# Transposes as a queue of single steps between projection matmuls, in place of groups of three to eight

## The chip, the cores and the metric

The kernel runs on one core of one Trainium2 chip. The metric is the device time of one execution in microseconds (us); the time of a kernel is the median of several executions. A difference of about 0.2% (4.6 us) is the least that a measurement of this kernel can tell from none.

## What is computed

A trunk of two decoder layers over 256 tokens of width 2048, in float32. Layer 0 mixes tokens with an mLSTM (four heads, value width 512), layer 1 with FoX attention (sixteen heads of width 128). Each layer then has a SwiGLU feed-forward block of inner width 5632, and a root-mean-square norm stands before each block and at the end:

```python
for layer in range(DEPTH):
    sh1, sc1, g1, sh2, sc2, g2 = split(silu(c) @ ada_w[layer] + ada_b[layer], 6)
    h = rms_norm(x, norm_mix_w[layer]) * (1.0 + sc1) + sh1
    y = mlstm_mixer(h, ...) if layer % 2 == 0 else fox_mixer(h, ...)
    x = x + g1 * y
    h = rms_norm(x, norm_ffn_w[layer]) * (1.0 + sc2) + sh2
    g, u = split(h @ w_gate_up[layer], 2)
    x = x + g2 * ((silu(g) * u) @ w_down[layer])
return rms_norm(x, final_norm_w)
```

## The kernel before

All weights are streamed from HBM once. `fetch` (L252) brings four blocks of 128 rows by 512 columns (1 MB) into one of five `raw` buffers. `split` (L257) makes of each half of it two float32r tiles: ScalarE casts `hi` (L263), VectorE computes the remainder `lo` (L264); `hi` and `lo` have four buffers each, and a half feeds two contraction steps. The activations are split in the same way, so a product is the sum of three float32r matmuls of 512 columns: `mm_t` (L287) does these three for one half of the tokens (L290, L291, L292), and `mm_a` calls it for both token halves. One fetch in `group_a` is therefore 8 calls of `mm_t`, 24 matmuls. Where the result is wanted with the tokens along the free axis, `mm_b` (L270) does the same with two matmuls, 512 columns (L273) and 256 columns (L276).

Some results come out with tokens on the partitions and are needed the other way round. TensorE turns them in blocks of 128 x 128: a transpose is a matmul with the block as the stationary operand and an identity matrix as the moving one. The places are `turned` (L342, four blocks into one PSUM bank, used for the SwiGLU output, L1093, and for the mLSTM queries and keys), `Norm.turn` (L478, four blocks of the normed residual, L485), `weights_t` (L889, three blocks of attention weights, L893), `emit` (L963, mLSTM output, L970) and `x_block` (L692, L695). After each group ScalarE and VectorE read the PSUM bank: for SwiGLU a cast (L1095) and a subtraction (L1096). The banks for this come from the pool `aux`, which has two.

What is not a projection waits in a list `steps` of jobs (transposes with their readers, attention scores, the mixing of a head). After each fetch `tick` (L242) calls `drain(adv)`, which settles outstanding PSUM copies and runs the next one or two jobs as a whole; then `bg` emits tiles of the adaLN modulation (`ada_tile`, L191): a DMA of 1 MB and one VectorE instruction over 2048 columns (L195). A `drain()` without a count runs all jobs that are left; one stands at the end of each of the two parts of a feed-forward block (6 and 5 groups of columns), before the down projection reads the activations. `carry_on` (L592) runs `Norm.rest` for one quarter of the columns ahead of a fetch.

The program is recorded in this order, and a scheduler then sets the order on each engine, except in the first part and in `bridge`, where it is by hand.

Of the kernel before, what the change touches and what calls it, by code (L numbers as in the profile page):

```python
# [31 lines left out]
def kernel(  # L32
# [201 lines left out]
    steps = []  # L234
    later = []

# [4 lines left out]
    def drain(n=None):  # L241
        if steps:  # L242
            settle()
        for _ in range(len(steps) if n is None else min(n, len(steps))):
            steps.pop(0)()
# [41 lines left out]
    def mm_t(ps, hi, lo, act, t, first, last):  # L287
# [4 lines left out]
        nc.tensor.matmul(ps, b, hi, start=False, stop=last, skip_group_check=True)  # L292

# [4 lines left out]
    def group_b(w, nk, c0, act, evac, bgn, adv=1):  # L298
        banks = [bank() for _ in range(4)]
        for k in range(0, nk, 4):  # L300
            ws = load_w(w, k, 4, c0)
            for m in range(4):
                cols = slice(m * P, (m + 1) * P)
                for j, (hi, lo) in enumerate(ws):
                    mm_b(
                        banks[m], hi[:, cols], lo[:, cols], act(k + j), k + j == 0, k + j == nk - 1
                    )
                if k + 4 == nk:
                    evac(m, banks[m])
# [33 lines left out]
    def turned(src, i):  # L343
        ps = abank()
        for j in range(2):
            for t in range(2):
# [3 lines left out]
                )  # L350
        return ps.rearrange("p (k t) -> p k t", t=T)
# [108 lines left out]
    class Norm:  # L460
# [62 lines left out]
        def rest(self, t, q):  # L523
            self.turn(t, q)
            self.affine(t, q)
# [66 lines left out]
    def carry_on(w2, hb, norm, rate):  # L592
        todo = [(0, 2), (1, 2), (0, 3), (1, 3)]

        def each(k):
            if todo:
                norm.rest(*todo.pop(0))
# [3 lines left out]
        for k in (4, 8):  # L601
            for n, (c, banks) in enumerate(hb.items()):
                group_a(w2, c, h_act, rate, ka=k, kb=k + 4, banks=banks, each=each if n < 2 else None)

# [87 lines left out]
    def x_block(t, j):  # L692
        ps = abank()
        for i in range(4):
            nc.tensor.transpose(  # L695
                ps[:, i * P : (i + 1) * P], xT[4 * j + i][:, t * P : (t + 1) * P], ident
            )
        nc.scalar.copy(X[:, t, 512 * j : 512 * (j + 1)], ps)

    ready_sqrt(eps_t)  # L700
    x_block(0, 0)
# [10 lines left out]
    x_block(1, 0)  # L712

    def row_scale():
# [9 lines left out]
        for t in range(2):  # L724
            x_block(t, 1)
# [157 lines left out]
    def act_tile(lst, k):  # L883
        return lst[k // 2][:, k % 2, :]
# [4 lines left out]
    def weights_t(W, WT):  # L889
        ps = abank()  # L890
        for i in range(3):
            cols = slice(i * P, (i + 1) * P)
            nc.tensor.transpose(ps[:, cols], W[:, cols], ident)  # L893
        nc.scalar.copy(WT, ps[:, : 3 * P])

    def mlstm_head(hd, q, k):
# [36 lines left out]
        def flip():  # L933
            weights_t(st["W"], st["WT"])
# [28 lines left out]
        def emit():  # L963
            yt = st["yt"]
            for i in range(2):
                y[2 * hd + i] = new_act()
                ps = abank()
                for j in range(2):
                    for t in range(2):
                        nc.tensor.transpose(  # L970
                            ps[:, j * T + t * P : j * T + (t + 1) * P],
                            yt[:, t, (2 * i + j) * P : (2 * i + j + 1) * P], ident,
                        )
                for j in range(2):
                    c = 4 * hd + 2 * i + j
                    dst = y[2 * hd + i][:, j, :]
                    src = ps[:, j * T : (j + 1) * T]
# [4 lines left out]
                    )  # L982

# [5 lines left out]
    def keep_t(c0, bgn, scale=None, adv=1, layer_w=0):  # L989
        if layer_w == 0:  # L990
# [5 lines left out]
            def flip():  # L996
                for i in range(2):
                    nc.scalar.copy(o[:, 2 * i : 2 * i + 2, :], turned(sp, i))
# [45 lines left out]
    def ffn(layer, begun, norm, rates, nsplit=0, srate=0.0, nxt=None):  # L1044
# [21 lines left out]
        for tq in quarters:  # L1066
            norm.rest(*tq)
# [13 lines left out]
        def swiglu(gr):  # L1081
# [10 lines left out]
            def flip(i):  # L1092
# [245 lines left out]
```

## Time and profile before

| | us |
|---|---|
| median of three runs (2296.80 to 2297.88) | 2297.38 |
| the profiled execution | 2300.83 |
| its span, first to last instruction | 2299.0 |
| PE (TensorE matmul) busy | 2275.4 |
| DVE (VectorE) busy | 1612.9 |
| ACT (ScalarE) busy | 1122.8 |

The granted TensorE clock is 1.00 in every stretch. In a row of the timeline the first number is the start, the second how long the record lasted. Matmuls overlap in the records (one that lasts 0.39 us is followed by the next after 0.23 us), so what a matmul costs is read from the starts: the time from one start to the next is called pitch below. PEld is the load of the stationary operand that each matmul has, in a row of its own. "[0.48 <-DVE ...]" at the end of a row is idle time before it and what ended it.

### The profile page before, as it was taken

Reading aid. Unit: us, or ns where it says so; the run is one execution under the profiler, and the core shown is the slowest. Engines: PE = TensorE matmul, PEld = TensorE weight load, DVE = VectorE, ACT = ScalarE, POOL = GpSimd, SP = SyncE. Lnnn points to the kernel's source line nnn. Section 1 sums busy time; section 2 is a strip of 40 time slices with the busy share of each in tenths; the row PEclk is TensorE's granted clock in tenths of the full one; section 3 lists DMA queues with packets and bytes.
Section 4 is the critical chain, followed back from the end, with each engine's and each line's share of the span. In section 5 each row is a group of like instructions: output and inputs, shape, how many; then the busy total and the mean of one; then the engine's idle time right before and its main releaser. Section 6 shows DMA issues by size and latency. Waiting matters only on the chain.

```text
span 2299.0 us, 26543 instructions
## 1 busy us (share of the span) xinstructions
PE 2275.4 (99%) x10376; PEld 1861.0 (81%) x10376; DVE 1612.9 (70%) x1829; ACT 1122.8 (49%) x1488; POOL 15.6 (1%) x40
## 2 busy tenths in 40 slices
PE   8999999999999999999999999999999999999998
PEld 4777878888888888888878888888888888888886
DVE  5998788878887878865687777777655554544554
ACT  3778664555543344444555444455444433444443
POOL 0000000000000000000000000000000000000000
PEclk9999999999999999999999999999999999999999
DMA  9998989798989889985667878775766555555552
GB/s 348 364 368 320 355 313 362 271 345 325 331 331 336 323 337 337 342 293 188 215 243 285 300 259 288 255 275 186 250 241 222 191 191 198 189 187 195 193 196 105
DMA packets 89090, 623.92 MB, mean 271 GB/s; under 512 B 10034, under 2 KB 10482, under 8 KB 14596
## 3 DMA queue, kind: packets, MB, share of 16 engines
q1 hardware_dynamic: 87552, 617.79, 74.3%
q0 software_dynamic: 1264, 4.29, 0.5%
q8 instruction: 81, 1.33, 0.2%
q14 instruction: 45, 0.37, 0.0%
q10 hardware_dynamic: 148, 0.14, 0.0%
HBM read 620.05 MB, written 2.13 MB: 271 GB/s over the span
## 4 chain that ended last, share of the span: by engine, by line
PE 88%; DVE 6%; DMA 3%; ACT 2%; issue 1%; SPq 0%; ACTq 0%; DVEq 0%
PE mm L292 25%; PE mm L291 25%; PE mm L290 25%; PE mm L273 5%; DVE ada L195 3%; PE mm L276 2%; DVE lo L264 2%; DMA ada<-in_ada_w_dram 2%; PE aux L347 1%; ACT hi L263 1%; DMA raw<-in_w_in_dram 1%; DMA slot<-in_w_in_dram 1%; PE aux L945 0%; PE aux L485 0%; PE aux L1144 0%
## 5 line engine op out<-in xcount | busy, mean ns | idle before, releaser
L264 DVE TENSOR_TENSOR lo<-raw,hi 128x1024 fp32r<-128x1024 f32 x764 | 926.9, 1223 | 556.8 <-ACT hi L263 556.2
L263 ACT CAST hi<-raw 128x1024 fp32r<-128x1024 f32 x764 | 797.1, 1053 | 920.3 <-PE mm L292 816.9
L291 PE MATMUL mm<-lo,hT 128*128 128x512 f32 x1840 | 718.3, 390 | 5.3 <-DVE lo L264 5.3
L290 PE MATMUL mm<-hi,hT 128*128 128x512 f32 x1840 | 719.3, 393 | 0.0
L292 PE MATMUL mm<-hi,hT 128*128 128x512 f32 x1840 | 718.1, 390 | 0.0
L195 DVE SCALAR_TENSOR_TENSOR ada<-ada,cs 128x2048 f32<-128x2048 f32 x192 | 438.9, 2286 | 49.2 <-DMA ada<-in_ada_w_dram 49.2
L291 PEld LDWEIGHTS mm<-lo,hT 128*128 128x128 f32 x1840 | 345.7, 188 | 80.1 <-DVE lo L264 10.2
L292 PEld LDWEIGHTS mm<-hi,hT 128*128 128x128 f32 x1840 | 345.4, 188 | 72.7 <-issue 0.5
L290 PEld LDWEIGHTS mm<-hi,hT 128*128 128x128 f32 x1840 | 345.3, 188 | 70.9 <-ACT hi L263 0.5
L290 PE MATMUL mm<-hi,slot 128*128 128x512 f32 x960 | 375.1, 391 | 0.2 <-ACT slot L978 0.2
L291 PE MATMUL mm<-lo,slot 128*128 128x512 f32 x960 | 374.4, 390 | 0.0
L292 PE MATMUL mm<-hi,slot 128*128 128x512 f32 x960 | 374.4, 391 | 0.0
L290 PEld LDWEIGHTS mm<-hi,slot 128*128 128x128 f32 x960 | 180.3, 188 | 37.7 <-ACT slot L978 0.8
L292 PEld LDWEIGHTS mm<-hi,slot 128*128 128x128 f32 x960 | 180.2, 188 | 37.6 <-issue 0.7
L291 PEld LDWEIGHTS mm<-lo,slot 128*128 128x128 f32 x960 | 180.2, 188 | 37.0
L273 PE MATMUL mm<-hT,hi 128*128 128x512 f32 x512 | 181.7, 402 | 0.6 <-DVE slot L359 0.6
L276 PE MATMUL mm<-hT,lo 128*128 128x256 f32 x512 | 138.3, 280 | 0.0
L273 PEld LDWEIGHTS mm<-hT,hi 128*128 128x128 f32 x512 | 94.4, 188 | 20.5 <-DVE slot L359 0.9
L276 PEld LDWEIGHTS mm<-hT,lo 128*128 128x128 f32 x512 | 96.6, 189 | 3.0
L800 ACT ACTIVATE slot<-mm 128x512 f32<-128x512 f32 x78 | 45.0, 593 | 33.9 <-PE mm L292 31.1
L435 ACT ACTIVATE t<-X 128x512 f32<-128x512 f32 x32 | 20.2, 631 | 39.2 <-DVE X L430 39.2
L1085 ACT ACTIVATE slot<-mm 128x512 f32<-128x512 f32 x44 | 25.4, 598 | 15.0 <-PE mm L292 13.8
(207 smaller groups left out, 980.5 us busy)
## 6 DMA issues: line engine op xcount, KB each, us to landing
ada<-in_ada_w_dram SPq DMA_DIRECT2D x192, 1024.0 KB, 6.5
raw<-in_gate_up_dram SPq DMA_DIRECT2D x176, 1024.0 KB, 4.9
raw<-in_down_dram SPq DMA_DIRECT2D x88, 1024.0 KB, 4.9
raw<-in_fox_in_dram SPq DMA_DIRECT2D x48, 1024.0 KB, 5.0
raw<-in_w_in_dram SPq DMA_DIRECT2D x44, 1024.0 KB, 7.3
raw<-in_w_out_dram SPq DMA_DIRECT2D x16, 1024.0 KB, 5.8
raw<-in_fox_out_dram SPq DMA_DIRECT2D x16, 1024.0 KB, 4.9
slot<-in_w_in_dram SPq DMA_DIRECT2D x16, 256.0 KB, 12.1
```

What stands on the lines that cost most here:

```text
L195: nc.vector.scalar_tensor_tensor(out=raw, in0=raw, scalar=1.0, in1=cs, op0=ALU.mult, op1=ALU.mult, accum_out=acc[layer][:, j : j + 1],)
L263: nc.scalar.copy(hi, raw[:, j : j + 2, :])
L264: nc.vector.tensor_tensor(lo, raw[:, j : j + 2, :], hi.bitcast(F32), op=ALU.subtract)
L273: nc.tensor.matmul(ps, hi, rhs, start=first, stop=last, skip_group_check=True)
L276: nc.tensor.matmul(ps[:, T:], lo, rhs[:, :T], start=False, stop=False, skip_group_check=True)
L290: nc.tensor.matmul(ps, a, hi, start=first, stop=False, skip_group_check=True)
L291: nc.tensor.matmul(ps, a, lo, start=False, stop=False, skip_group_check=True)
L292: nc.tensor.matmul(ps, b, hi, start=False, stop=last, skip_group_check=True)
L347: nc.tensor.transpose(ps[:, j * T + t * P : j * T + (t + 1) * P], src[:, t, (2 * i + j) * P : (2 * i + j + 1) * P], ident,)
L435: nc.scalar.activation(t512(), X[:, t, 512 * i : 512 * (i + 1)], AF.Square, accum_out=self.ss[:, t, i : i + 1],)
L800: nc.scalar.activation(SP[i][:, t, :], banks[t], func)
L1085: nc.scalar.activation(sg[:, t, :], banks[t], AF.Silu)
```

## The change

Jobs become generators. `drain(n)` no longer runs jobs but moves them to a list `active`; `poke()` advances the first of them by one step, and `mm_t` calls it after its three matmuls, `mm_b` after every second pair. Each transpose in `turned`, `weights_t`, `x_block` and `Norm.rest` is followed by a `yield`, so at most one transpose comes between two calls of `mm_t`; the readers of the PSUM bank are emitted one poke after the last transpose. `act_tile` forces jobs to their end when a projection asks for an activation that is not there yet, and for that the lists of activations are filled only when a tile is complete. The `drain()` ahead of the down projection is gone. `emit` uses `turned`. Jobs that are no generators (scores, mix) run whole at one poke. `carry_on` has a `drain()` ahead of each round and at its end. No computation and no transfer is added or removed, and on each engine the counts of instructions by kind are the same.

```diff
@@ -232,17 +232,40 @@
             bg(1.0)
 
     steps = []
+    active = []
     later = []
+
+    def run(f):
+        g = f()
+        if g is not None:
+            yield from g
+
+    def now(g):
+        for _ in g:
+            pass
+
+    def poke():
+        if active and next(active[0], None) is None:
+            active.pop(0)
+
+    def force():
+        if not active:
+            settle()
+            active.append(run(steps.pop(0)))
+        now(active.pop(0))
 
     def settle(n=0):
         while len(later) > n:
             later.pop(0)()
 
     def drain(n=None):
+        if n is None:
+            while active or steps:
+                force()
+            return
         if steps:
             settle()
-        for _ in range(len(steps) if n is None else min(n, len(steps))):
-            steps.pop(0)()
+        active.extend(run(steps.pop(0)) for _ in range(min(n, len(steps))))
 
     def tick(n, adv=1):
         drain(adv)
@@ -290,6 +313,7 @@
         nc.tensor.matmul(ps, a, hi, start=first, stop=False, skip_group_check=True)
         nc.tensor.matmul(ps, a, lo, start=False, stop=False, skip_group_check=True)
         nc.tensor.matmul(ps, b, hi, start=False, stop=last, skip_group_check=True)
+        poke()
 
     def mm_a(ps, hi, lo, act, first, last):
         for t in range(2):
@@ -305,6 +329,8 @@
                     mm_b(
                         banks[m], hi[:, cols], lo[:, cols], act(k + j), k + j == 0, k + j == nk - 1
                     )
+                    if j % 2:
+                        poke()
                 if k + 4 == nk:
                     evac(m, banks[m])
             tick(bgn, adv)
@@ -348,6 +374,7 @@
                     ps[:, j * T + t * P : j * T + (t + 1) * P],
                     src[:, t, (2 * i + j) * P : (2 * i + j + 1) * P], ident,
                 )
+                yield True
         return ps.rearrange("p (k t) -> p k t", t=T)
 
     def total(ps, out, scale=None):
@@ -521,7 +548,13 @@
             self.low(t, q)
 
         def rest(self, t, q):
-            self.turn(t, q)
+            src = self.x[t, q // 2][:, 512 * (q % 2) : 512 * (q % 2) + 512]
+            ps = abank()
+            for j in range(4):
+                cols = slice(j * P, (j + 1) * P)
+                nc.tensor.transpose(ps[:, cols], src[:, cols], ident)
+                yield True
+            self.ps[t, q] = [ps]
             self.affine(t, q)
 
     def bridge(w, row0, nk, c0, act, res, i, norm, w2, heads, rate=0.0):
@@ -594,13 +627,15 @@
 
         def each(k):
             if todo:
-                norm.rest(*todo.pop(0))
+                active.append(norm.rest(*todo.pop(0)))
             if todo:
                 norm.scale(*todo[0])
 
         for k in (4, 8):
+            drain()
             for n, (c, banks) in enumerate(hb.items()):
                 group_a(w2, c, h_act, rate, ka=k, kb=k + 4, banks=banks, each=each if n < 2 else None)
+        drain()
 
     def scratch(n):
         tiles = []
@@ -695,10 +730,11 @@
             nc.tensor.transpose(
                 ps[:, i * P : (i + 1) * P], xT[4 * j + i][:, t * P : (t + 1) * P], ident
             )
+            yield True
         nc.scalar.copy(X[:, t, 512 * j : 512 * (j + 1)], ps)
 
     ready_sqrt(eps_t)
-    x_block(0, 0)
+    now(x_block(0, 0))
     ssb = bank()
     parts = [sq[:, T * i : T * (i + 1)] for i in range(4)] + [s_end]
     for t in range(2):
@@ -709,7 +745,7 @@
             )
     r0 = small([P, 2], "rstd")
     nc.scalar.activation(r0, ssb[:, :2], AF.Sqrt, bias=eps_t, scale=1.0 / D)
-    x_block(1, 0)
+    now(x_block(1, 0))
 
     def row_scale():
         nc.vector.reciprocal(r0, r0)
@@ -722,7 +758,7 @@
         nc.tensor.matmul(ps[:, :T], ones, dg, start=True, stop=True)
         nc.scalar.copy(R, ps[:, :T])
         for t in range(2):
-            x_block(t, 1)
+            now(x_block(t, 1))
 
     w = w_in
     COLS = [2048 + 512 * i for i in range(8)] + [0, 1024, 512, 1536]
@@ -881,6 +917,8 @@
     y = [None] * 8
 
     def act_tile(lst, k):
+        while lst[k // 2] is None:
+            force()
         return lst[k // 2][:, k % 2, :]
 
     def new_act():
@@ -891,6 +929,7 @@
         for i in range(3):
             cols = slice(i * P, (i + 1) * P)
             nc.tensor.transpose(ps[:, cols], W[:, cols], ident)
+            yield True
         nc.scalar.copy(WT, ps[:, : 3 * P])
 
     def mlstm_head(hd, q, k):
@@ -931,7 +970,7 @@
             st["r"] = r
 
         def flip():
-            weights_t(st["W"], st["WT"])
+            yield from weights_t(st["W"], st["WT"])
 
         def mix():
             r, WT = st["r"], st["WT"]
@@ -963,23 +1002,18 @@
         def emit():
             yt = st["yt"]
             for i in range(2):
-                y[2 * hd + i] = new_act()
-                ps = abank()
-                for j in range(2):
-                    for t in range(2):
-                        nc.tensor.transpose(
-                            ps[:, j * T + t * P : j * T + (t + 1) * P],
-                            yt[:, t, (2 * i + j) * P : (2 * i + j + 1) * P], ident,
-                        )
+                ps = yield from turned(yt, i)
+                new = new_act()
                 for j in range(2):
                     c = 4 * hd + 2 * i + j
-                    dst = y[2 * hd + i][:, j, :]
-                    src = ps[:, j * T : (j + 1) * T]
+                    dst = new[:, j, :]
+                    src = ps[:, j, :]
                     nc.scalar.activation(dst[:, :T], src, AF.Copy, scale=nw_hs[:, c : c + 1])
                     nc.vector.scalar_tensor_tensor(
                         out=dst[:, T:], in0=src, scalar=nw_hs[:, c : c + 1],
                         in1=dst[:, :T].bitcast(F32), op0=ALU.mult, op1=ALU.subtract,
                     )
+                y[2 * hd + i] = new
 
         return [scores, flip, mix, emit]
 
@@ -995,7 +1029,7 @@
 
             def flip():
                 for i in range(2):
-                    nc.scalar.copy(o[:, 2 * i : 2 * i + 2, :], turned(sp, i))
+                    nc.scalar.copy(o[:, 2 * i : 2 * i + 2, :], (yield from turned(sp, i)))
 
             steps.append(flip)
             return o
@@ -1064,7 +1098,7 @@
         flush()
         drain()
         for tq in quarters:
-            norm.rest(*tq)
+            now(norm.rest(*tq))
         if nsplit:
             want(0, G2)
             want(1, SC1, SH1)
@@ -1089,15 +1123,16 @@
             first = len(acts)
             acts.extend([None, None])
 
-            def flip(i):
-                acts[first + i] = dst = new_act()
-                ps = turned(sg, i)
+            def flip(acts, i):
+                ps = yield from turned(sg, i)
+                dst = new_act()
                 nc.scalar.copy(dst[:, :, :T], ps)
                 nc.vector.tensor_tensor(
                     dst[:, :, T:], ps, dst[:, :, :T].bitcast(F32), op=ALU.subtract
                 )
-
-            steps.extend([lambda: flip(0), lambda: flip(1)])
+                acts[first + i] = dst
+
+            steps.extend([lambda a=acts, i=i: flip(a, i) for i in range(2)])
 
         act = lambda k: act_tile(acts, k)
         for ci, ch in enumerate(chunks):
@@ -1105,7 +1140,6 @@
             rate = rates[2 * ci]
             for gr in ch:
                 swiglu(gr)
-            drain()
             rate = rates[2 * ci + 1]
             end = ci == len(chunks) - 1
             res = Residual(layer, G2, end)
@@ -1131,6 +1165,7 @@
     f_raw = slot()[:, : KT * 16].rearrange("p (k c) -> p k c", c=16)
     nc.scalar.dma_start(f_raw, fox_gates)
     y = [None] * 8
+    half = [None] * 8
     vals = {}
 
     def fox_head(hd, q, k):
@@ -1166,12 +1201,12 @@
                 nc.vector.tensor_scalar(wt, wt, sm[:, t : t + 1], None, op0=ALU.mult)
 
         def flip():
-            weights_t(st["W"], st["WT"])
+            yield from weights_t(st["W"], st["WT"])
 
         def mix():
             v, WT = vals[hd // 4][:, :, hd % 4 * P : (hd % 4 + 1) * P], st["WT"]
             if hd % 2 == 0:
-                y[hd // 2] = new_act()
+                half[hd // 2] = new_act()
             O = abank()
             nc.tensor.matmul(
                 O[:, :T], v[:, 0, :], WT[:, :T], start=True, stop=False, skip_group_check=True
@@ -1179,7 +1214,9 @@
             nc.tensor.matmul(
                 O[:, P:T], v[:, 1, :], WT[:, T:], start=False, stop=True, skip_group_check=True
             )
-            split_act(O[:, :T], act_tile(y, hd))
+            split_act(O[:, :T], act_tile(half, hd))
+            if hd % 2:
+                y[hd // 2] = half[hd // 2]
 
         return [scores, flip, mix]
```

In both programs TensorE has 458 transposes. Before they stand in 104 runs, 55 of them of four and 14 of eight; after in 307 runs, of which 274 are a single transpose. Most of those still in groups are in the hand-ordered `bridge`, in the first 100 us and with the mLSTM heads, where jobs are forced.

TensorE, the first SwiGLU output of layer 0 that is turned; `slot_812_4288` holds it, `mm_842` and `mm_843` are the two banks of the projection that runs meanwhile. Before:

```order
L291 MATMUL mm_843_4452<-lo_848_4462,hT_134 128x512
L292 MATMUL mm_843_4452<-hi_847_4461,hT_134 128x512
L347 MATMUL aux_850_4490<-ident_81,slot_812_4288 128x128 x4
L290 MATMUL mm_842_4451<-hi_852_4499,hT_134 128x512
```

After (L313 to L315 are the lines that were L290 to L292, L373 was L347):

```order
L315 MATMUL mm_842_4451<-hi_850_4491,hT_134 128x512
L373 MATMUL aux_854_4502<-ident_81,slot_812_4288 128x128
L313 MATMUL mm_843_4452<-hi_850_4491,hT_134 128x512
L314 MATMUL mm_843_4452<-lo_851_4492,hT_134 128x512
L315 MATMUL mm_843_4452<-hi_850_4491,hT_134 128x512
L373 MATMUL aux_854_4502<-ident_81,slot_812_4288 128x128
L313 MATMUL mm_842_4451<-hi_850_4491,hT_134 128x512
L314 MATMUL mm_842_4451<-lo_851_4492,hT_134 128x512
L315 MATMUL mm_842_4451<-hi_850_4491,hT_134 128x512
L373 MATMUL aux_854_4502<-ident_81,slot_812_4288 128x128
```

The four transposes now stand three matmuls apart.

ScalarE, a little later in the same stage: casts of weights (`hi`), of turned activations (L1095, after: L1129), the SiLU that empties two projection banks (L1085, after: L1119) and copies that seed the banks of a later projection (L326, after: L352). Before:

```order
L263 CAST hi_864_4554<-raw_861_4548 128x1024
L1095 CAST slot_849_4489<-aux_850_4490 128x2x256
L263 CAST hi_868_4587<-raw_867_4585 128x1024
L263 CAST hi_870_4591<-raw_867_4585 128x1024
L1095 CAST slot_856_4531<-aux_857_4532 128x2x256
L1085 ACTIVATE slot_841_4450<-mm_842_4451 128x512
L1085 ACTIVATE slot_841_4450<-mm_843_4452 128x512
```

After:

```order
L286 CAST hi_868_4587<-raw_867_4585 128x1024
L1129 CAST slot_855_4519<-aux_854_4502 128x2x256
L1119 ACTIVATE slot_841_4450<-mm_842_4451 128x512
L352 COPY mm_889_4711<-slot_717_3769 128x512
L1119 ACTIVATE slot_841_4450<-mm_843_4452 128x512
L286 CAST hi_870_4591<-raw_867_4585 128x1024
```

The cast of the second half of a fetch (`hi_870_4591`) now stands behind four instructions that stood behind it or ahead of its first half.

TensorE again, the end of the first part of the feed-forward block of layer 0, where the down projection (`slot_849_4489` is its first activation) begins. Before:

```order
L290 MATMUL mm_1022_5421<-hi_1024_5424,slot_849_4489 128x512
L291 MATMUL mm_1022_5421<-lo_1025_5425,slot_849_4489 128x512
L347 MATMUL aux_1018_5405<-ident_81,slot_969_5149 128x128
L347 MATMUL aux_1020_5413<-ident_81,slot_969_5149 128x128
L292 MATMUL mm_1022_5421<-hi_1024_5424,slot_849_4489 128x512
L290 MATMUL mm_1021_5420<-hi_1024_5424,slot_849_4489 128x512
L347 MATMUL aux_1018_5405<-ident_81,slot_969_5149 128x128 x3
```

After:

```order
L315 MATMUL mm_1018_5405<-hi_1022_5412,slot_865_4570 128x512
L313 MATMUL mm_1017_5404<-hi_1026_5445,slot_887_4693 128x512
L314 MATMUL mm_1017_5404<-lo_1027_5446,slot_887_4693 128x512
L315 MATMUL mm_1017_5404<-hi_1026_5445,slot_887_4693 128x512
L373 MATMUL aux_1030_5456<-ident_81,slot_969_5149 128x128
```

The last SwiGLU output of the part (`slot_969_5149`) was turned among the first seven matmuls of the down projection; now its first transpose comes after the first fetch of it, 22 matmuls later. On SyncE's queue only the two loads of `final_norm_w` near the end move, behind two or three further fetches of `down`.

## The prediction

> **What bounds the kernel now.** I read the page first: the span, the busy shares and the chain that ended last.
>
> ```profile
> span 2299.0 us, 26543 instructions
> PE 2275.4 (99%) x10376; PEld 1861.0 (81%) x10376; DVE 1612.9 (70%) x1829; ACT 1122.8 (49%) x1488; POOL 15.6 (1%) x40
> PE 88%; DVE 6%; DMA 3%; ACT 2%; issue 1%; SPq 0%; ACTq 0%; DVEq 0%
> ```
>
> TensorE carries 88% of the chain, and its records leave 23.6 us of the span uncovered. A covered span need not be full work, since the records overlap, so the next view is the timeline of TensorE in a plain stretch of the down projection, first and last of 55 matmuls from 1099.75 to 1111.99:
>
> ```profile
> 1099.75 0.39 PE L291 MATMUL mm<-lo,slot 128*128 128x512 f32 x1
> ...
> 1111.99 0.39 PE L291 MATMUL mm<-lo,slot 128*128 128x512 f32 x1
> ```
>
> 12.24 us over 54 steps is a pitch of 0.2267 us for 512 columns. There is no gap in this stretch, so each matmul or transpose that is put into TensorE's queue moves the end by what it adds to these starts. The third view is the list of TensorE's waits from 226 us on (before that the kernel fills its pipeline, and the order of that part does not change on any engine):
>
> ```profile
> PE mm L291 <- DVE lo L264: 1.0, 1, 1.0
> PE mm L556 <- DVE hT L510: 0.9, 1, 0.9
> PE mm L273 <- DVE slot L359: 0.6, 1, 0.6
> PE aux L347 <- DVE slot L1088: 0.5, 1, 0.5
> PE aux L485 <- DVE slot L474: 0.2, 1, 0.2
> PE aux L945 <- DVE slot L979: 0.2, 1, 0.2
> PE mm L290 <- ACT slot L978: 0.2, 1, 0.2
> ```
>
> That is 3.6 us in seven waits over 2073 us. TensorE's own queue is the bound. So the change can do two things: alter what a transpose costs in TensorE's pipeline, or create and remove waits, of which there is little to remove.
>
> **A transpose in a group and alone.** A group of four, between two ordinary matmuls:
>
> ```profile
> 575.11 0.39 PE L292 MATMUL mm<-hi,hT 128*128 128x512 f32 x1
> 575.34 0.60 PE L347 MATMUL aux<-ident,slot 128*128 128x128 f32 x4
> 575.69 0.48 PE L290 MATMUL mm<-hi,hT 128*128 128x512 f32 x1
> 576.00 0.40 PE L291 MATMUL mm<-lo,hT 128*128 128x512 f32 x1
> ```
>
> From the start of the matmul ahead to the start of the second one behind are 0.89 us. Two matmuls at 0.2267 would take 0.453, so the group costs 0.437 us, 0.109 per transpose. The matmul behind must be counted in: its record starts early and lasts 0.48 in place of 0.39, because part of the last transpose's price is shown there. Transposes that stand alone exist in this trace too, and they decide the matter. One has a narrow stationary operand (16 columns, the modulation vectors at 336 us), one the full block (at 351 us, with the mLSTM heads):
>
> ```profile
> 336.40 0.39 PE L290 MATMUL mm<-hi,slot 128*128 128x512 f32 x1
> 336.62 0.27 PE L400 MATMUL aux<-ident,mods 128*16 128x128 f32 x1
> 336.65 0.47 PE L291 MATMUL mm<-lo,slot 128*128 128x512 f32 x1
> 336.96 0.40 PE L292 MATMUL mm<-hi,slot 128*128 128x512 f32 x1
> ```
>
> ```profile
> 350.96 0.39 PE L292 MATMUL mm<-hi,slot 128*128 128x512 f32 x1
> ...
> 351.42 0.40 PE L291 MATMUL mm<-lo,slot 128*128 128x512 f32 x1
> 351.66 0.27 PE L970 MATMUL aux<-ident,slot 128*128 128x128 f32 x1
> 351.69 0.48 PE L292 MATMUL mm<-hi,slot 128*128 128x512 f32 x1
> 352.00 0.40 PE L290 MATMUL mm<-hi,slot 128*128 128x512 f32 x1
> ```
>
> By the same sum the first costs 0.56 - 0.453 = 0.107 us and the second 0.58 - 0.453 = 0.127. The neighbours of the second are themselves slow, two of them taking 0.46 (350.96 to 351.42); against these it costs 0.12. So a lone transpose is no cheaper than one in a group, at 0.107 to 0.127 against 0.109. I take 0.113: the full block is the right shape but its place is disturbed, and the other is undisturbed, as the places are where the SwiGLU outputs are turned.
>
> The Trainium skill speaks against the change here ("TensorE: Matmul & The Clock Gate", LDWEIGHTS): loading a stationary operand takes its 128 columns over 1.2 GHz, an estimate of 107 ns. The trace agrees, with 0.109 per transpose in a group. By that rule the matmul behind a lone transpose still waits for its own load, which a transpose of 128 columns is too short to hide, and the sum would be nought in place of the small loss below.
>
> **The terms of the sum.**
>
> Single transposes: in the order of the changed kernel 274 of 458 transposes stand alone. 274 x (0.113 - 0.109) = +1.1 us. The bounds are 274 x (0.107 - 0.109) = -0.5 and 274 x (0.127 - 0.109) = +4.9.
>
> The end of the first part of layer 0's feed-forward block, where the `drain()` goes. TensorE, and the VectorE instruction that it waited for:
>
> ```profile
> 695.38 0.39 PE L291 MATMUL mm<-lo,slot 128*128 128x512 f32 x1
> 696.25 0.44 PE L347 MATMUL aux<-ident,slot 128*128 128x128 f32 x2 [0.48 <-DVE slot L1088]
> 695.50 1.28 DVE L1088 TENSOR_TENSOR slot<-mm,slot 128x512 f32<-128x512 f32 x2
> ```
>
> From 695.38 to 696.25 are 0.87 us where 0.23 would do: 0.64 us lost. In the new order the first of these transposes comes 22 matmuls later, 5.0 us, long after the products end at 696.8, so the wait goes whole: -0.6 us. Nothing else is late there, since the down projection starts with activations that were turned long before. The list of waits has only one such row, so the other three ends of parts give nothing.
>
> Waits that remain: the four of the list that name L264, L510, L359 and L474 belong to weights and to the hand-ordered bridge, which the change leaves. The two of 0.2 with the heads may go or grow by as much; I put them at nought, -0.4 to +0.4.
>
> Readers of the banks: two casts and two subtractions per SwiGLU column group, as before, now up to twelve matmuls (2.7 us) later. The activation is read by the down projection, which needs the last turned outputs of a part only in its last fetch, so nobody waits. The two `aux` banks are held longer, but jobs run one after another and a fetch has eight pokes for the five that a turning needs. The attention weights of layer 1 (L893) are read by their head's `mix` 26 projection matmuls or more after the last transpose, but for one head where the order stays as it was. The moved loads of `final_norm_w` are used only after three more rounds of the down projection. These are nought, because TensorE's queue has other work ahead of each reader.
>
> The sum is +1.1 - 0.6 = +0.5 us against the profiled execution, whose span is 2299.0. The execution took 2300.83, 3.5 more than the median of 2297.38; I put the same difference on the median: 2297.9.
>
> **The rivals.** First, a lone transpose could hide what in a group is exposed, and then cost only what its moving columns cost. The pitch of a matmul of half the columns bounds that price:
>
> ```profile
> 1280.81 0.28 PE L276 MATMUL mm<-hT,lo 128*128 128x256 f32 x1
> 1280.93 0.40 PE L273 MATMUL mm<-hT,hi 128*128 128x512 f32 x1
> ```
>
> 256 columns take 0.12, so 128 would take 0.06 if columns were all: 274 x (0.109 - 0.06) = 13.4 us less, 2284.5. For it speaks only that no lone transpose of a SwiGLU output has been seen; against it stand both rows above. The Trainium skill's page of the same title (Back-to-back issue gap) has 56 ns for 128 columns when a matmul's load is hidden, which would give much the same; the lone transpose at 0.107 does not agree.
>
> Second, slower: the weights could come late, because the casts of `hi` now stand behind other work in ScalarE's queue. In layer 0's feed-forward block (400 to 700 us), grouped by line, ScalarE and VectorE:
>
> ```profile
> L263 ACT CAST hi<-raw 128x1024 fp32r<-128x1024 f32 x102 | 107.3, 1055 | 110.1 <-PE mm L292 98.8 <-issue 6.7 <-ACT mm L326 2.8
> L326 ACT COPY mm<-slot 128x512 f32<-128x512 f32 x22 | 12.4, 592 | 0.0
> L1095 ACT CAST slot<-aux 128x512 fp32r<-128x512 f32 x12 | 6.9, 580 | 1.8 <-PE aux L347 1.8
> L1085 ACT ACTIVATE slot<-mm 128x512 f32<-128x512 f32 x12 | 6.5, 598 | 0.0
> L264 DVE TENSOR_TENSOR lo<-raw,hi 128x1024 fp32r<-128x1024 f32 x102 | 124.1, 1223 | 47.1 <-ACT hi L263 47.0
> L195 DVE SCALAR_TENSOR_TENSOR ada<-ada,cs 128x2048 f32<-128x2048 f32 x38 | 86.8, 2285 | 3.3 <-DMA ada<-in_ada_w_dram 3.3
> L1096 DVE TENSOR_TENSOR slot<-aux,slot 128x512 fp32r<-128x512 f32 x12 | 8.1, 683 | 0.0
> ```
>
> Today the casts wait for TensorE (98.8 us) to free one of four buffers, so they run as far ahead as they can. When one comes free, three halves of 12 matmuls are still to do: 36 x 0.2267 = 8.2 us of cover. In the new order the cast of a second half stands behind a cast of activations, two SiLU and one seed copy: 0.58 + 2 x 0.60 + 0.59 + 1.05 = 3.4 us to its end. Then VectorE, with one modulation tile and one subtraction ahead, 2.29 + 0.68 + 1.22 = 4.2. That is 7.6 of 8.2. The point from which it decides is a second modulation tile in the same gap: 7.6 + 2.29 is 1.7 us over. With 38 such tiles to 102 halves that can't be the rule, but if it happened once in each of the six column groups of this stretch it would cost 6 x 1.7 = 10 us: 2308. Against it: VectorE sat idle for 47 us here, waiting for the casts, so there is room to catch up.
>
> Third, that the change does not do what it says: excluded for most of it, as the order shows 274 single transposes; with the mLSTM heads and in the bridge they stay in groups, which is counted above.
>
> **How the numbers follow.** The forecast, no change to be measured, has 0.82; its own bounds are 2297.4 - 0.5 - 0.6 - 0.4 - 0.5 = 2295.4, the last 0.5 being half the spread of the runs before, and 2297.4 + 4.9 - 0.6 = 2301.7. The first rival has 0.09, the second 0.09. The range of 8 in 10 is the forecast's own, 2295.4 to 2301.7, which leaves the rivals out. A measurement of this kernel can tell about 0.2%, 4.6 us (below 2292.8, above 2302.0), so faster has 0.09, the same 0.82, slower 0.09.
>
> **What would show it.** Right: in the timeline after, a lone transpose adds 0.11 us between the matmul ahead and the second behind; the wait on L1088 is gone from TensorE's list, and no row of more than 1 us has come. The first rival would show 0.06 at that place. The second would show a wait of TensorE for `lo` between 400 and 1160 us that repeats with the column groups, and less than 98.8 us of the casts' waiting for TensorE. The forecast is wrong if the time leaves the bounds while lone transposes still cost 0.11, for then the waits have moved in a way that I have not seen.

## The result, and the profile after

The changed kernel is slower: 2309.88 us (median; 2306.54 to 2311.26) against 2297.30 (2296.80 to 2297.88) for the kernel before, a ratio of 1.0053 with a 95% interval of 1.0035 to 1.0070. The forecast was 2297.9, the top of its range 2301.7.

The page of the profile after, its span, busy times and chain:

```profile
span 2304.7 us, 26534 instructions
PE 2276.9 (99%) x10376; PEld 1854.0 (80%) x10376; DVE 1613.2 (70%) x1829; ACT 1123.6 (49%) x1488; POOL 15.6 (1%) x40
PE 89%; DVE 5%; DMA 2%; ACT 2%; issue 1%; SPq 0%; ACTq 0%; DVEq 0%
```

Busy times and the chain are almost as they were, so the page does not show where the time went. The first three rows of the list of TensorE's waits do, again from 226 us on (total, number, longest):

```profile
PE aux L373 <- DVE slot L996: 3.3, 2, 3.1
PE mm L589 <- DVE hT L537: 2.4, 2, 1.8
PE aux L512 <- DVE slot L501: 2.0, 2, 1.3
```

Before it had seven rows, none over 1.0 us. Now one wait lasts 3.1 us, and two in the bridge 1.8 and 1.3. (L373 was L347 and L970, L996 was L957, L589 was L556, L537 was L510, L512 was L485, L501 was L474.) The row with L1088 is gone, as forecast.

To see what each place costs, the matmuls of the projections (those of the gates among them), which stand in the same order in both programs, are matched by their number, counted from 0. Start of some of them:

| matmul of a projection, by number | before, us | after, us | after later by |
|---|---|---|---|
| 700 | 209.54 | 206.07 | -3.5 |
| 1140 | 334.13 | 330.77 | -3.4 |
| 1200, behind the mLSTM heads | 353.37 | 354.31 | 0.9 |
| 1500 | 421.51 | 422.40 | 0.9 |
| 1750, behind the first bridge | 482.29 | 486.03 | 3.7 |
| 9423, near the end | 2239.09 | 2244.90 | 5.8 |

The execution of before that was profiled got going 3.5 us later, so its span hides that much of the loss. From number 700 on the change costs 9.3 us: 4.3 at the heads, 2.8 in the bridge, 2.1 in the 1760 us behind it, 0.1 elsewhere. This is the profiled execution's own distance from the median of before: 2306.54 - 2297.30 = 9.2.

**The heads.** VectorE's order around the normalisation of the third mLSTM head's output, with the numbers of the rows (`ada` are modulation tiles, `lo` remainders of weights, `hrs` and `slot_2528` or `slot_2554` the head). Before:

```
280 L195 SCALAR_TENSOR_TENSOR ada_2766,acc_124<-ada_2766,cs 128x2048
281 L930 RECIPROCAL r_2433<-r_2433 128x2
282 L954 RECIPROCAL hrs_2530<-hrs_2530 128x2
283 L955 TENSOR_TENSOR hrs_2530<-hrs_2530,r_2415 128x2
284 L957 SCALAR_TENSOR_TENSOR slot_2528<-aux_2531,hrs_2530,slot_541 128x512
285 L957 SCALAR_TENSOR_TENSOR slot_2528<-aux_2534,hrs_2530,slot_541 128x512
286 L264 TENSOR_TENSOR lo_2736<-raw_2729,hi_2735 128x1024
```

After:

```
280 L195 SCALAR_TENSOR_TENSOR ada_2766,acc_124<-ada_2766,cs 128x2048
281 L969 RECIPROCAL r_2452<-r_2452 128x2
282 L287 TENSOR_TENSOR lo_2736<-raw_2729,hi_2735 128x1024
283 L195 SCALAR_TENSOR_TENSOR ada_2803,acc_124<-ada_2803,cs 128x2048
284 L993 RECIPROCAL hrs_2556<-hrs_2556 128x2
285 L287 TENSOR_TENSOR lo_2772<-raw_2769,hi_2771 128x1024
286 L994 TENSOR_TENSOR hrs_2556<-hrs_2556,r_2431 128x2
287 L287 TENSOR_TENSOR lo_2776<-raw_2769,hi_2775 128x1024
288 L996 SCALAR_TENSOR_TENSOR slot_2554<-aux_2557,hrs_2556,slot_541 128x512
289 L996 SCALAR_TENSOR_TENSOR slot_2554<-aux_2560,hrs_2556,slot_541 128x512
```

The job `mix` of this head now waits in `active` and is emitted a little later, and the scheduler has put three `lo` and a modulation tile ahead of the head's result, among them `lo` of the next fetch. What this does is read from three engines. The timeline of VectorE after:

```profile
336.47 1.20 DVE L287 TENSOR_TENSOR lo<-raw,hi 128x1024 fp32r<-128x1024 f32 x1
337.60 0.15 DVE L994 TENSOR_TENSOR hrs<-hrs,r 128x2 f32<-128x2 f32 x1
338.42 1.23 DVE L287 TENSOR_TENSOR lo<-raw,hi 128x1024 fp32r<-128x1024 f32 x1 [0.68 <-ACT hi L286]
339.56 1.40 DVE L996 SCALAR_TENSOR_TENSOR slot<-aux,hrs,slot 128x512 f32<-128x512 f32 x2
```

ScalarE's cast for the second of these `lo`:

```profile
337.34 1.04 ACT L286 CAST hi<-raw 128x1024 fp32r<-128x1024 f32 x1 [1.66 <-PE mm L315]
```

And TensorE, which takes its queue in order:

```profile
336.92 0.39 PE L315 MATMUL mm<-hi,slot 128*128 128x512 f32 x1
340.36 0.43 PE L373 MATMUL aux<-ident,slot 128*128 128x128 f32 x1 [3.06 <-DVE slot L996]
341.02 1.75 PE L373 MATMUL aux<-ident,slot 128*128 128x128 f32 x7 [0.23 <-DVE slot L996]
342.49 0.80 PE L313 MATMUL mm<-hi,slot 128*128 128x512 f32 x1
343.08 0.63 PE L314 MATMUL mm<-lo,slot 128*128 128x512 f32 x1
```

Read backwards: the transposes wait for L996; L996 stands behind a `lo` that waits for its cast; the cast needs a buffer that TensorE's last matmul ahead of the transposes frees (337.31). So nothing of the 1.04 + 1.23 us and the first half of L996 runs beside TensorE. The transposes start at 340.36 where 336.92 + 0.23 = 337.15 was free: 3.2 us. Before, VectorE had done the same work in time, though only just, as its timeline and TensorE's show:

```profile
335.76 1.41 DVE L957 SCALAR_TENSOR_TENSOR slot<-aux,hrs,slot 128x512 f32<-128x512 f32 x2
337.09 1.22 DVE L264 TENSOR_TENSOR lo<-raw,hi 128x1024 fp32r<-128x1024 f32 x1
```

```profile
337.24 1.09 PE L970 MATMUL aux<-ident,slot 128*128 128x128 f32 x8
```

L957 ended at 337.17 and the transposes began at 337.24. A margin of 0.07 us is no row in a list of waits, and it is hardly one at all: after, the second transpose starts 0.06 us behind the end of L996 (339.56 + 1.40 = 340.96, and 341.02).

The other 1.1 of the 4.3 us come behind the wait. Three stretches of the span after: behind the length stands the busy time of PE, PEld, DVE, ACT and POOL, each with its number of instructions, then TensorE's granted clock, and last what the DMA did:

```profile
337.05:340.46 3.41, 0.35 (x3) 0.10 (x1) 2.73 (x5) 1.04 (x1) 0.00 (x0) 1.00 1.01 426
340.46:343.88 3.42, 3.19 (x11) 2.48 (x12) 3.42 (x6) 1.22 (x3) 0.00 (x0) 0.50 1.01 426
343.88:347.29 3.41, 3.41 (x13) 1.99 (x12) 3.22 (x5) 1.37 (x4) 0.00 (x0) 1.00 0.94 344
```

Having stood still for 3.1 us, TensorE gets half its clock for 3.4: seven transposes take 341.02 to 342.49, 0.21 each, and 512 columns 0.43 (343.08 to 343.51) in place of 0.2267.

**The bridge.** Its order is by hand, but modulation tiles are not part of it: the scheduler sets them between its instructions. Before it set two there, after three. Two of the three, with what stands behind them, on VectorE after:

```profile
426.39 2.28 DVE L195 SCALAR_TENSOR_TENSOR ada<-ada,cs 128x2048 f32<-128x2048 f32 x1
428.60 0.69 DVE L457 TENSOR_TENSOR X<-X,t 128x512 f32<-128x512 f32 x1
430.60 0.49 DVE L501 TENSOR_SCALAR slot<-X,rstd 128x512 f32<-128x512 f32 x1
433.56 2.28 DVE L195 SCALAR_TENSOR_TENSOR ada<-ada,cs 128x2048 f32<-128x2048 f32 x1
435.76 0.68 DVE L537 TENSOR_TENSOR hT<-t,hT 128x512 fp32r<-128x512 f32 x1
```

And TensorE, which waits for L501 and for L537:

```profile
431.14 1.09 PE L512 MATMUL aux<-ident,slot 128*128 128x128 f32 x8 [1.29 <-DVE slot L501]
436.50 1.19 PE L589 MATMUL mm<-slot,hT 128*128 128x512 f32 x4 [1.77 <-DVE hT L537]
```

One tile stands ahead of the residual `X` that the norm waits for, one ahead of the last subtraction of a norm quarter. Before, the tile at this place came behind `X`, while VectorE had nothing else to do:

```profile
425.61 0.69 DVE L430 TENSOR_TENSOR X<-X,t 128x512 f32<-128x512 f32 x1
426.22 2.29 DVE L195 SCALAR_TENSOR_TENSOR ada<-ada,cs 128x2048 f32<-128x2048 f32 x1
```

### The profile page after: what moved, and what is told of

It is laid out like the page before. It is cut to its first block, busy times and chain, and to the rows that moved or that the text cites. A ratio compares the mean times of both kernels' runs of the same rounds, so it can differ in the third digit from the quotient of the medians.

```text
span 2304.7 us, 26534 instructions
## 1 busy us (share of the span) xinstructions
PE 2276.9 (99%) x10376; PEld 1854.0 (80%) x10376; DVE 1613.2 (70%) x1829; ACT 1123.6 (49%) x1488; POOL 15.6 (1%) x40
## 4 chain that ended last, share of the span: by engine, by line
PE 89%; DVE 5%; DMA 2%; ACT 2%; issue 1%; SPq 0%; ACTq 0%; DVEq 0%
PE mm L315 25%; PE mm L313 25%; PE mm L314 25%; PE mm L296 5%; PE mm L299 3%; DVE ada L195 3%; DVE lo L287 2%; DMA ada<-in_ada_w_dram 2%; PE aux L373 1%; ACT hi L286 1%; PE aux L984 0%; PE aux L1179 0%; PE mm L589 0%; PE mm L585 0%; PE aux L1211 0%
## 5 line engine op out<-in xcount | busy, mean ns | idle before, releaser
L313 PE MATMUL mm<-hi,hT 128*128 128x512 f32 x1840 | 733.8, 401 | 0.0
L315 PE MATMUL mm<-hi,hT 128*128 128x512 f32 x1840 | 718.9, 391 | 0.0
L313 PEld LDWEIGHTS mm<-hi,hT 128*128 128x128 f32 x1840 | 345.6, 188 | 82.8 <-ACT slot L836 0.2
L315 PEld LDWEIGHTS mm<-hi,hT 128*128 128x128 f32 x1840 | 345.4, 188 | 73.7 <-issue 0.5
L313 PE MATMUL mm<-hi,slot 128*128 128x512 f32 x960 | 379.1, 395 | 0.0
L315 PE MATMUL mm<-hi,slot 128*128 128x512 f32 x960 | 374.2, 390 | 0.0
L313 PEld LDWEIGHTS mm<-hi,slot 128*128 128x128 f32 x960 | 180.6, 188 | 39.2 <-issue 0.5
L315 PEld LDWEIGHTS mm<-hi,slot 128*128 128x128 f32 x960 | 180.3, 188 | 37.9 <-DVE slot L1012 0.4
L373 PE MATMUL aux<-ident,slot 128*128 128x128 f32 x240 | 60.3, 278 | 3.3 <-DVE slot L996 3.3
L836 ACT ACTIVATE slot<-mm 128x512 f32<-128x512 f32 x78 | 45.3, 595 | 33.8 <-PE mm L315 30.7
L373 PEld LDWEIGHTS aux<-ident,slot 128*128 128x128 f32 x240 | 33.3, 143 | 13.3 <-DVE slot L996 4.3
```

Of the source, the lines that this page charges most:

```text
L313: nc.tensor.matmul(ps, a, hi, start=first, stop=False, skip_group_check=True)
L373: nc.tensor.transpose(ps[:, j * T + t * P : j * T + (t + 1) * P], src[:, t, (2 * i + j) * P : (2 * i + j + 1) * P], ident,)
L836: nc.scalar.activation(SP[i][:, t, :], banks[t], func)
```

## The experiments

The theory that these rows suggest is one of order: the lone transposes cost almost nothing, and the loss is four VectorE instructions ahead of the head's result and tiles ahead of two results in the bridge. The rival is one of price: each lone transpose costs more than a place in a group, 12.6 / 274 = 0.046 us more, all along the kernel, and the waits only change places. (The table speaks against it already: 16 lone transposes lie between numbers 700 and 1140, and the loss there is 0.1 us in all.) In each kernel the line numbers are its own.

**Half the change each.** A switch decides whether jobs run step by step or whole, as before, and it is turned at the start of the first feed-forward block:

```diff
-        active.extend(run(steps.pop(0)) for _ in range(min(n, len(steps))))
+        for _ in range(min(n, len(steps))):
+            if single[0]:
+                active.append(run(steps.pop(0)))
+            else:
+                now(run(steps.pop(0)))
...
-                active.append(norm.rest(*todo.pop(0)))
+                if single[0]:
+                    active.append(norm.rest(*todo.pop(0)))
+                else:
+                    now(norm.rest(*todo.pop(0)))
...
+    single[0] = True
```

This one has 258 of the lone transposes, all behind the bridge:

> The changed kernel, but with whole jobs (groups) up to the end of the first bridge and single transposes only from the feed-forward block of layer 0 on; TensorE's order up to there is that of the kernel before, and 258 of the 274 lone transposes stay. Order theory (the loss comes from VectorE's order among the mLSTM heads, where TensorE waits 3.1 us for L996, and in the bridge at 430 us): the 4.3 and 2.9 us lost there are gone, so about 2302.7, 2299 to 2304. Price theory (each lone transpose costs more than in a group, 12.6 us / 274 = 0.046 each): 258 x 0.046 = 11.9 above before, 2309.

Measured: 2299.72 us against 2298.15 for the kernel before in the same job, 1.6 more; ratio 1.0006 (0.9997 to 1.0015). TensorE's longest waits from 226 us on:

```profile
PE mm L594 <- DVE hT L542: 0.3, 1, 0.3
PE aux L517 <- DVE slot L506: 0.2, 1, 0.2
```

The rival would have it at 258 x 0.046 = 11.9 us more. It falls.

The other half, with the switch the other way round: `single` begins as `True`, and the feed-forward block starts with `drain()` and `single[0] = False`. It has 16 lone transposes that stood in groups before:

> The other half: single transposes up to the end of the first bridge, whole jobs after it; 16 lone transposes are left and VectorE's order with the heads is that of the changed kernel. Order theory: 4.3 + 2.9 = 7.2 above before, about 2304.5, with the waits on L996 and in the bridge at their places. Price theory: 16 x 0.046 = 0.7 above before, 2298.

Measured: 2306.28 us, 8.1 more than before; ratio 1.0036 (1.0023 to 1.0049). The wait at the heads is there in full, and so is the 1.3 of the bridge, though not its 1.8:

```profile
PE aux L378 <- DVE slot L1004: 3.4, 2, 3.1
PE aux L517 <- DVE slot L506: 2.3, 2, 1.3
PE mm L594 <- DVE hT L542: 0.7, 2, 0.5
```

So the time is lost where almost no lone transpose is.

**The same instructions, put back by hand.** All steps stay single. The `lo` that are the 94th to 96th of the program and the 55th modulation tile (282, 283, 285 and 287 in the order above) are queued on VectorE behind the head's result:

```diff
+    behind = {("lo", 94): "head", ("lo", 95): "head", ("lo", 96): "head", ("ada", 55): "head"}
...
-        nc.vector.tensor_tensor(lo, raw[:, j : j + 2, :], hi.bitcast(F32), op=ALU.subtract)
+        with placed("lo"):
+            nc.vector.tensor_tensor(lo, raw[:, j : j + 2, :], hi.bitcast(F32), op=ALU.subtract)
...
+            if hd == 2:
+                anchor["head"] = last.ins
```

> The changed kernel with four VectorE instructions (three lo, one modulation tile) forced behind the normalisation of mLSTM head 2, where they stood before; transposes as in the changed kernel. Order theory: the wait on L996 goes, 4.3 us less than the changed kernel, about 2305.6. Price theory: no change, 2309.9.

Measured: 2303.95 us, 5.8 more than before; ratio 1.0023 (1.0014 to 1.0033). Four instructions in another place take 6.8 of the 12.6 us, more than the 4.3 expected. The wait of 3.1 us at the third head is gone; one of 0.7 for ScalarE has come a little behind it (at 341 us), and the last row belongs to the next head, at 353 us. The bridge waits as it did:

```profile
PE mm L600 <- DVE hT L548: 2.7, 3, 1.8
PE aux L523 <- DVE slot L512: 1.7, 2, 1.3
PE mm L324 <- ACT slot L1024: 0.7, 1, 0.7
PE aux L384 <- DVE slot L1007: 0.5, 2, 0.3
```

By the matmuls' numbers the heads lose 1.4 us here and the bridge 2.9, and the clock falls nowhere between the heads and the end of the work. How much of the 6.8 us is a clock that no longer falls in the executions without a profile is not shown.

Then two modulation tiles of the bridge as well, the 66th and 67th, queued behind its last subtraction of the first norm half (`("ada", 66): "bridge", ("ada", 67): "bridge"`):

> As the run with the head's order put back, and two more modulation tiles forced behind the hand-ordered part of the first bridge. Order theory: 7.2 us less than the changed kernel, about 2302.7, and no wait of more than 0.5 us in the bridge at 430 us. Price theory: 2309.9.

Measured: 2299.89 us, 1.7 more than before; ratio 1.0005 (0.9995 to 1.0014). The largest waits that are left:

```profile
PE mm L324 <- ACT slot L1024: 0.7, 1, 0.7
PE aux L384 <- DVE slot L1007: 0.5, 2, 0.3
```

With six VectorE instructions back behind the results that TensorE waits for, the kernel with all its lone transposes can't be told from the kernel before.

**The changed kernel again**, to have its size beside the next three:

> The changed kernel once more, beside the kernels of this call on the same chip. Both theories: about 12 us above the kernel before, 2309 to 2311; if the true size is what the two halves gave one by one (8.1 + 1.6 us), 9.7 above, 2308.

Measured: 2311.28 us (2309.19 to 2315.25) against 2297.68, 13.6 more; ratio 1.0059 (1.0044 to 1.0074). In this execution the clock fell behind the bridge too, which it had not done in the first profile. Its stretches there, read as above:

```profile
433.95:437.36 3.41, 1.63 (x8) 1.02 (x7) 3.41 (x6) 3.41 (x6) 0.00 (x0) 1.00 0.01 2
437.36:440.78 3.42, 3.42 (x9) 2.65 (x10) 3.42 (x4) 0.72 (x1) 0.00 (x0) 0.50 0.98 314
```

By the matmuls' numbers the bridge lost 4.5 us here and 2.8 in the first profile, with the same waits; the difference, 1.7, is half of the 3.42 us at half clock. The heads lost 4.7 and 4.3.

**The late start alone.** No transpose is single: a poke runs a whole job. Only the start of a job moves, from the end of a fetch to the pokes of the next one:

```diff
     def poke():
-        if active and next(active[0], None) is None:
-            active.pop(0)
+        if active:
+            now(active.pop(0))
```

> The changed kernel with one line different: a poke runs the first job to its end, so transposes stand in groups again, but jobs still start one fetch later than before. VectorE's order with the heads and in the first bridge is that of the changed kernel (three lo and a modulation tile ahead of head 2's normalisation). Order theory: the loss stays without any lone transpose, 8 us above the kernel before, with TensorE's wait on L996 of about 3 us. Price theory, and the theory that single transposes spread the work too thin: as before, 2298.

Measured: 2307.00 us, 9.3 more than before; ratio 1.0035 (1.0022 to 1.0048). On VectorE the order is that of the changed kernel up to the end of the first bridge, and so are the waits:

```profile
PE aux L373 <- DVE slot L996: 3.2, 2, 3.1
PE mm L589 <- DVE hT L537: 2.4, 2, 1.8
PE aux L512 <- DVE slot L501: 2.0, 3, 1.3
```

Not the single steps but the list `active`, which makes a job wait for the next poke, moves the head's result in the order.

**The `drain()` alone.** The switch of the first experiment, never turned on: every job whole and at its old time, but no `drain()` ahead of the down projection.

> The changed kernel with whole jobs run at once, as before, everywhere: what stays of the change is that the drain ahead of the down projection is gone. TensorE's order is that of the kernel before up to there. Both theories: the wait of 0.6 us at 695 us goes and nothing else, 2297.5 where the kernel before has 2298.1.

Measured: 2296.81 us, 0.9 less than before; ratio 0.9998 (0.9989 to 1.0007). The sign is the expected one, the size can't be told from nothing.

**Which of the four at the head.** Only the three `lo` go behind the head's result, the modulation tile stays free (`behind` without `("ada", 55)`):

> The changed kernel with only the three lo forced behind head 2's normalisation; the modulation tile (2.3 us) stays ahead of it. If the wait of 3.1 us is the modulation tile's length, at least 2 us of it stay. If it is the lo, which wait for casts that wait for TensorE to free buffers, it goes, and the time falls as with all four put back, 6 us below the changed kernel.

Measured: 2300.17 us, 2.5 more than before; ratio 1.0014 (1.0005 to 1.0024). TensorE at the heads:

```profile
336.94 0.39 PE L326 MATMUL mm<-hi,slot 128*128 128x512 f32 x1
337.18 1.03 PE L384 MATMUL aux<-ident,slot 128*128 128x128 f32 x8
338.85 0.50 PE L324 MATMUL mm<-hi,slot 128*128 128x512 f32 x1 [0.64 <-ACT slot L1024]
```

The transposes start 0.24 us behind the matmul ahead, without a wait. So it is the `lo`, whose cast needs TensorE to go on, and not the length of the modulation tile. As a whole this kernel comes out better than the one with all four moved back, because the scheduler set the bridge's tiles otherwise in it as well:

```profile
PE aux L523 <- DVE slot L512: 1.0, 2, 0.8
PE mm L600 <- DVE hT L548: 0.6, 1, 0.6
```

Its time is therefore no measure of the head alone; its rows at the head are.

**What stays open.** The halves give 8.1 + 1.6 = 9.7 us, the whole 12.6 and 13.6. Both halves lack the `drain()`, so the 0.9 us that its absence may save is in their sum twice: 10.6. Part of the rest is the clock, whose fall behind the bridge cost 1.7 us in one profile of the whole and did not come in the other. The smaller wait that the half with 16 lone transposes has in the bridge (0.7 us in the row of its last subtraction, where the whole has 2.4) is no part of it. There the clock was at 0.50 from 433.49 to 436.90, so TensorE came to that place later and waited less, and the bridge lost 2.9 us by the matmuls' numbers, as much as in the first profile of the whole. Behind the bridge the whole lost 2.1 and 2.7 us in its two profiles, the halves together 0.6, or 1.5 without counting the `drain()` twice; what the last 0.6 to 1.2 us are is not shown. How the longer executions, up to 2315.25 us, are made up is not shown, since no profile lies above 2309.49.

## Why the prediction failed, step by step

- **TensorE's own queue is the bound; a change can alter a price or move waits.** Right, and the second is what happened.
- **A lone transpose adds 0.113 us, against 0.109 in a group: +1.1.** Right in its mechanism, small in its size. TensorE in the feed-forward block after:

```profile
579.65 0.39 PE L315 MATMUL mm<-hi,hT 128*128 128x512 f32 x1
579.88 0.27 PE L373 MATMUL aux<-ident,slot 128*128 128x128 f32 x1
579.91 0.48 PE L313 MATMUL mm<-hi,hT 128*128 128x512 f32 x1
580.23 0.39 PE L314 MATMUL mm<-lo,hT 128*128 128x512 f32 x1
```

  580.23 - 579.65 - 0.453 = 0.127 here, by these rounded starts; over some 180 such places of the two feed-forward blocks the mean is 0.120, and over some 35 groups of four before 0.111 each. 274 x 0.009 = 2.5 us in place of 1.1, inside the bounds. The half with 258 lone transposes took 1.6 more than before, and 2.5 if the 0.9 that the missing `drain()` may save is added. The mean lies between the two places of before, 0.107 and 0.127, that the term was drawn from; 0.113 leaned too far to the narrow block.
- **The wait on L1088 goes: -0.6.** Right: the row is gone in every kernel without that `drain()`, and alone this is worth 0.9 less, within its noise.
- **"Waits that remain: the four of the list that name L264, L510, L359 and L474 belong to weights and to the hand-ordered bridge, which the change leaves. The two of 0.2 with the heads may go or grow by as much."** This is the step that failed. The change leaves the hand-written order, but not what the scheduler fills in between. In the first bridge the wait of 0.2 us on L474 became one of 1.3, and one of 1.8 on the last subtraction came where there was none; the 0.9 on L510 belongs to a later bridge, at 1161 us, and is 0.6 there after. And the wait that costs most was none before: at the heads L957 was 0.07 us early. The working took the list of waits for a list of the places at risk, but it shows only those that were already late. The order of VectorE at the heads was open to reading beforehand, and rows 282 to 287 show four instructions in front of the head's result. (The range was also too narrow by its own terms: its lower end holds the 0.4 of these waits and 0.5 for the spread of the runs, its upper end neither. With both it would be 2302.6, still far below 2309.88.)
- **Readers of the banks: nought.** Right for the SwiGLU outputs: in the kernel with 258 lone transposes, TensorE's list from 226 us on has only four rows of 0.2 to 0.3, all of the heads and the bridge. For the heads the term only asked when TensorE reads the result, and not what now stands ahead of the result on VectorE.
- **First rival, a lone transpose hides: 2284.5.** Refuted by the 0.120 above, not 0.06.
- **Second rival, a modulation tile in the gap and weights late in layer 0's feed-forward block: 2308.** Near in size, wrong in place. ScalarE between 400 and 700 us after:

```profile
L286 ACT CAST hi<-raw 128x1024 fp32r<-128x1024 f32 x102 | 107.2, 1054 | 109.7 <-PE mm L315 104.1 <-ACT mm L352 2.8 <-DVE mods L187 1.7
```

  The casts wait for TensorE for 104.1 us, against 98.8 before; the rival needed less. What it got right is the kind of mechanism, VectorE holding up TensorE with work that is not urgent. That happened at the heads and in the bridge, not in the column groups where it was looked for.
- **"The forecast is wrong if the time leaves the bounds while lone transposes still cost 0.11, for then the waits have moved in a way that I have not seen."** This is what happened.

## What to carry to other kernels

When a change alters at what time jobs are handed to a scheduler, read the new order of the engines that feed the bound engine at every place where it waits or is barely served, the untouched ones too: a result that was ready 0.07 us early is as exposed as one that was late. The dangerous neighbour is not the longest one but the one that itself waits for the bound engine, as a `lo` behind a cast behind a freed buffer does, since then nothing of the chain runs beside it. And where an order is by hand, background work that the scheduler may insert needs its place by hand too.

## What the runs showed of the hardware

A standstill of TensorE costs more than its length. At the heads 3.1 us without work were followed by 3.4 us at a granted clock of 0.50 (transposes 0.21 us apart in place of 0.11, 512 columns 0.43 in place of 0.2267), which added 1.1 us to the 3.2 of the wait.

When the clock falls can be read from the trace's own record of it. In every profile of this case each fall comes a whole number of steps of 3.413 us after the moment at which the clock was first full: 94 steps in the first profile of the changed kernel (19.61 to 340.46 us), 93 and 121 in the second (24.35 to 341.79 and 437.36). From 226 us to the last projections there are seven falls in the ten profiles. Six lasted one step and one lasted two, with the late start alone at the heads (339.58 to 346.41 us).

The Trainium skill ("TensorE: Matmul & The Clock Gate", What's actually happening) puts the fall behind at least one idle window of about 3.4 us, and the windows run free of the kernel. The traces agree with the length and with the free run. But the steps ahead of the falls were not idle from end to end. In the second profile TensorE worked for 1.63 us of the step ahead of the fall in the bridge (433.95 to 437.36, above), and for 0.78 of the one at the heads:

```profile
338.38:341.79 3.41, 0.78 (x5) 0.59 (x6) 3.05 (x4) 0.32 (x1) 0.00 (x0) 1.00 1.01 425
341.79:345.20 3.41, 3.41 (x11) 2.41 (x10) 3.33 (x7) 1.82 (x4) 0.00 (x0) 0.50 1.02 430
```

Ahead of the seven falls TensorE was busy for 0.35 to 1.75 us of a step, and from 226 us to the last projections no step with less than 1.75 went without a fall; one with 1.75 did (429.21 to 432.62 in the first profile). So the border lies near half a step. Busy time alone is not the whole rule, since early in one profile, at 34 us, a step with 1.53 us had no fall.

This is why the same waits cost a fall in one execution and none in the next. In the bridge of the first profile the waits of 1.3 and 1.8 us fell into steps that were busy for 1.75 and 2.11 us, and the clock stayed at 1.00; in the second the wait of 1.8 lay whole in one step. At the heads the fall came 0.1 us behind the first transpose in the first profile and 1.1 us behind it in the second. Where the steps lie differs from execution to execution, so the price of a wait of this length can't be forecast for one execution.
